# The first microseconds of a six-layer stack on one core: loading order, held loads and products of ones

## The chip, the cores and the metric

The kernel is one program on one NeuronCore of a Trainium2 chip. Its time is the device time of one execution in microseconds (us); lower is better. The span is the stretch from the first to the last instruction that the hardware profiler recorded in one such execution. Engines are named as in the profile: PE (matrix products; PEld are its weight loads), DVE (vector engine), ACT (scalar engine), POOL (GpSimd), SP (the engine that here only issues transfers). ACTq and SPq are those engines' instruction queues, POOLq the transfers that POOL issues.

## The reference, cut to what matters

A residual of 272 tokens (16 learned ones and 256 of the input) by 1024 features passes four layers (attention, mLSTM, HGRN2, attention) and then two layers of a second block. Only the entry into layer 0 bears on the change:

```python
u = rmsnorm(h, norm_gain[i])                       # h: 272 x 1024, fp32
q, k, v, z = _split(u @ w_in, (A_W, A_KVW, A_KVW, A_W))   # w_in: 1024 x 2560, fp32
q = rope(rmsnorm(q.reshape(bsz, lp, A_HEADS, A_HD), q_gain), pos)
k = rope(rmsnorm(k.reshape(bsz, lp, A_KV, A_HD), k_gain), pos)
...
h = h + jnp.where(valid[None, :, None], y, 0.0)
```

All inputs are fp32, and the products are to be of fp32 quality.

## The kernel before, in words

**Products in three passes.** Each fp32 operand is split into a rounded part (`hi`, the type fp32r) and the rest (`lo`). A block of 128 by 128 weights costs three products: hi by hi (L397), hi by the residual's lo (L398), lo by the residual's hi (L399). The residual's two halves are `XH` (written by ACT, L540) and `XL` (DVE, L528), one pair of instructions for each of the eight blocks k of 128 features; the residual itself, `HT`, comes in four transfers of two blocks each.

**Weights in parts.** The weights of the whole program lie in one array in the order of use and are read in parts of 128 partitions by 1024 columns (512 KB), which are eight blocks and so 24 products. I number the parts of layer 0 from 0. A part gets its two halves in one of two ways:
- *raw*: SP loads it to `wraw` (L258, three buffers), ACT rounds it to `whi` (L384), DVE subtracts to `wlo` (L390). Parts 0 to 5 of layer 0 go this way; parts 4 and 5 into the buffers MH and ML in place of whi and wlo.
- *by POOL*: POOL issues a transfer that rounds on its way into `whi` (L330, the "rounding load"), ACT writes its negative to `wlo` (L339), and POOL issues a second transfer of the same weights that adds onto it (L340). Parts from 6 on go this way. The rounding load is issued five parts ahead (`HI_AHEAD`), the second one three parts ahead (`LO_AHEAD`); `whi` has seven buffers, `wlo` five.

**The start.** SP issues, in this order, the small constants `sm`, HT blocks 0-1, part 0, HT 2-3, HT 4-5, part 1, HT 6-7, then tables of constants (`ce` with the rotary tables, `ca`), part 2, further tables, part 3 (L262, L258, `PRE`). POOL issues the rounding load of part 6 at once. ACT loads its table, makes XH and the squares `nsq` of the norm (L475), POOL adds the squares (`nsa`, L486), and two products with ones (L490, L491) give the sum for every token. The output tile of part 0 needs all eight blocks of XH and XL. The instructions are put in order on each engine by a scheduling layer that goes by the program's order and its own idea of when data are there; `Flow` (class `Flow`) places the attention's steps between the products by counted units of work.

**What follows the start.** Tile 0 (part 0) is a key tile, tiles 1 to 4 are queries. Their results pass ACT (square L690 or L737, scaled copy L692 or L740), a swap of halves by two transfers that ACT issues (`sw`, L589), DVE (rotary products L746 to L748) and the norm of the heads (L700, L702 and the Newton steps L440 to L444). At the middle of part 8 stand the short scores of the 16 learned tokens (L789), which wait for the last rotated queries (L748).

**Weights of later layers.** As soon as a raw buffer is free, SP loads the next raw part, which after part 5 belongs to layer 1.

Of the kernel before, what the change touches and what calls it, by code (L numbers as in the profile page):

```python
# [18 lines left out]
P = 128  # L19
# [29 lines left out]
PRE = (0, 4)  # L49
# [174 lines left out]
def kernel(ctx: ExitStack, tc: tile.TileContext, xt: bass.AP, pos: bass.AP, small: bass.AP,  # L224
# [19 lines left out]
    seq = order or _tile_order()  # L244
    acc = {}
# [5 lines left out]
    def load_raw(c0, n):  # L251

        t, kt, nt = seq[state["i"]]
        w = _cols(kt, nt)
        acc["nraw"] = acc.get("nraw", 0) + 1
        own = acc["raws"] if t[0] in "fd" and acc["nraw"] % 2 and "raws" in acc else wp
        raw = own.tile([P, SUB * P], F32, name="wraw", bufs=WR)
        nc.sync.dma_start(raw[:, :n], wts[state["off"]:state["off"] + P * w].rearrange("(p c) -> p c", p=P)[:, c0:c0 + n])  # L258
        return raw

    for k in range(0, KD, 2):
        nc.sync.dma_start(HT[:, k:k + 2, :], xt[:, k:k + 2, :])  # L262
        if stages[0] == 0 and len(raws) < len(PRE) and k == PRE[len(raws)]:
            raws.append(load_raw(len(raws) * SUB * P, SUB * P))
# [59 lines left out]
    def begin_parts(p):  # L324

        while parted and parted[0][0] <= p:
# [3 lines left out]
            nc.gpsimd.dma_start(hi[:, :c1 - c0], src)  # L330
# [23 lines left out]
    def chunk(tag, into=None, more_due=False):  # L354
# [6 lines left out]
        for c0 in range(0, n, SUB * P):  # L361
# [5 lines left out]
            if not more_due:  # L367
                begin_parts(p + HI_AHEAD)
# [3 lines left out]
            raw = raws.pop(0) if raws else load_raw(c0, c1 - c0)  # L372
# [8 lines left out]
            with ExitStack() as es:  # L381
                if (tag, state["n"], c0 // (SUB * P)) in HELD and "last" in acc:
                    es.enter_context(tc.issue_after(acc["last"]))
                nc.scalar.copy(hi[:, :c1 - c0], raw[:, :c1 - c0])  # L384
            with ExitStack() as es:
                if more and "lo" in acc:
                    es.enter_context(tc.issue_after(acc["lo"]))
                elif tag[0] == "f" and (state["n"], c0) == CH and "R" in acc:
                    es.enter_context(tc.issue_after(acc["R"]))
                V.tensor_tensor(lo[:, :c1 - c0], raw[:, :c1 - c0], hi[:, :c1 - c0].bitcast(F32), op=ALU.subtract)  # L390
# [102 lines left out]
    def keep_warm(src, n):  # L493

        ps = mx("s")
        for _ in range(n):
            PE.matmul(ps[:, :P], ones, src[:, :P], start=True, stop=True)
# [95 lines left out]
    class Flow:  # L593
# [29 lines left out]
        def run(self, gen):  # L623
            for w in gen:
                self.unit(w)

# [1504 lines left out]
```

## Time and profile before

| | us |
|---|---|
| median of 3 runs | 1443.03 |
| the runs | 1437.77, 1443.72, 1443.03 |
| the profiled execution | 1443.98 |
| its span | 1442.2 |
| PE busy in the span | 1365.0 (95%) |
| DVE / ACT / POOL busy | 988.1 / 770.1 / 445.6 |
| first product of the span starts at | 10.61 |

Some 1.8 us of the profiled execution lie outside of its span. A time in a row of the timeline is counted from the span's start; the second figure is how long the instruction took, and the brackets tell for how long the engine had been idle and what ended that. A product that streams 272 columns is listed with its whole passage, but the next one starts 0.125 us later at the full clock of 2.4 GHz and 0.227 us later at half of it; the granted clock in the windows is 1.00 and 0.50 for these two. "DMA" is the mean busy share of the 16 transfer engines; because packets overlap it can pass 1.

### The profile page before, as it was taken

The numbers are of one execution on the slowest core, as the hardware profiler recorded it, in microseconds if no ns is written. First come the engines' busy times: TensorE is split into PE (matmuls) and PEld (weight loads), VectorE is DVE, ScalarE is ACT, GpSimd is POOL, SyncE is SP. The second block draws the span as 40 slices with busy tenths as digits, with TensorE's granted clock in tenths as the row PEclk, the third lists the DMA queues.
The fourth block names the chain that finished last, engine by engine and source line by source line (L and its number), as shares of the span: only waits on it lengthen the run. The fifth ranks groups of instructions, "written<-read, shape, count | busy, mean of one in ns | idle before, by whom it ended". The sixth has DMA issues, their size and how long they took to land.

```text
span 1442.2 us, 27480 instructions
## 1 busy us (share of the span) xinstructions
PE 1365.0 (95%) x10347; PEld 1268.9 (88%) x10347; DVE 988.1 (69%) x2419; ACT 770.1 (53%) x1621; POOL 445.6 (31%) x611
## 2 busy tenths in 40 slices
PE   6999999999899999998999999999998998999998
PEld 5878999999899888897688888999998877899986
DVE  5765579999866666767655676787545665677754
ACT  5576655556635455455764656454444555455432
POOL 3222378778605333132214512100005430400000
PEclk9999999999999999999999999999999999999999
DMA  9988999999469988469879963566557975366662
GB/s 299 280 183 206 238 251 250 240 235 239 123 199 238 233 180 187 117 199 263 198 158 260 274 168 95 161 203 192 179 185 201 245 189 139 93 192 195 193 190 88
DMA packets 85493, 287.03 MB, mean 199 GB/s; under 512 B 10368, under 2 KB 16200, under 8 KB 85360
## 3 DMA queue, kind: packets, MB, share of 16 engines
q0 software_dynamic: 44512, 160.74, 48.2%
q1 hardware_dynamic: 34272, 118.60, 25.6%
q10 hardware_dynamic: 6576, 5.94, 1.5%
q8 instruction: 81, 1.33, 0.4%
q14 instruction: 52, 0.43, 0.1%
HBM read 279.01 MB, written 1.07 MB: 194 GB/s over the span
## 4 chain that ended last, share of the span: by engine, by line
PE 68%; DVE 13%; DMA 9%; ACT 4%; issue 3%; POOL 2%; ACTq 0%; DVEq 0%; SPq 0%; POOLq 0%
PE pmm L397 14%; PE pmm L398 13%; PE pmm L399 13%; DVE wlo L390 2%; PE ps L399 2%; PE ps L398 2%; PE ps L397 2%; DMA sw<-qg 2%; DMA wraw<-in_wts_dram 2%; DMA wlo<-in_wts_dram 2%; DMA sw<-qr 1%; DMA whi<-in_wts_dram 1%; PE pa L873 1%; PE ps L833 1%; DMA sw<-krr 1%
## 5 line engine op out<-in xcount | busy, mean ns | idle before, releaser
L397 PE MATMUL pmm<-XH,whi 128*128 128x272 f32 (+1 forms) x1544 | 460.3, 299 | 23.0 <-ACT whi L384 10.6
L398 PE MATMUL pmm<-XL,whi 128*128 128x272 f32 (+1 forms) x1544 | 447.2, 290 | 3.0 <-DVE XL L528 3.0
L399 PE MATMUL pmm<-XH,wlo 128*128 128x272 f32 (+1 forms) x1544 | 447.1, 290 | 2.4 <-DMA wlo<-in_wts_dram 1.9
L384 ACT CAST whi<-wraw 128x1024 fp32r<-128x1024 f32 (+1 forms) x211 | 218.0, 1033 | 237.9 <-DMA wraw<-in_wts_dram 195.9
L397 PEld LDWEIGHTS pmm<-XH,whi 128*128 128x128 f32 x1544 | 296.7, 192 | 36.8 <-ACT whi L384 10.6
L390 DVE TENSOR_TENSOR wlo<-wraw,whi 128x1024 fp32r<-128x1024 f32 (+1 forms) x211 | 256.2, 1216 | 87.7 <-PE pmm L399 36.1
L398 PEld LDWEIGHTS pmm<-XL,whi 128*128 128x128 f32 x1544 | 297.1, 192 | 4.6 <-DVE XL L528 4.0
L399 PEld LDWEIGHTS pmm<-XH,wlo 128*128 128x128 f32 x1544 | 297.2, 193 | 3.4 <-DMA wlo<-in_wts_dram 2.1
L339 ACT ACTIVATE wlo<-whi 128x1024 fp32r<-128x1024 f32 (+1 forms) x150 | 157.9, 1054 | 91.1 <-PE pmm L399 46.3
L330 POOL DMA_DIRECT2D whi<-in_wts_dram x150 | 88.5, 591 | 342.8 <-PE pmm L399 292.2
L397 PE MATMUL pmm<-MH,whi 128*128 128x256 f32 (+1 forms) x624 | 183.3, 294 | 0.6 <-DVE HT L961 0.6
L340 POOL DMA_DIRECT2D wlo<-in_wts_dram x150 | 130.2, 871 | 164.3 <-ACT wlo L339 93.4
L398 PE MATMUL pmm<-ML,whi 128*128 128x256 f32 (+1 forms) x624 | 179.2, 287 | 1.5 <-DVE ML L581 0.9
L399 PE MATMUL pmm<-MH,wlo 128*128 128x256 f32 (+1 forms) x624 | 178.4, 286 | 0.0
L397 PEld LDWEIGHTS pmm<-MH,whi 128*128 128x128 f32 x624 | 119.0, 191 | 7.9 <-issue 6.5
L398 PEld LDWEIGHTS pmm<-ML,whi 128*128 128x128 f32 x624 | 119.0, 191 | 2.2 <-DVE ML L581 1.1
L399 PEld LDWEIGHTS pmm<-MH,wlo 128*128 128x128 f32 x624 | 119.3, 191 | 0.0
L398 PE MATMUL ps<-XL,whi 128*128 128x256 f32 (+1 forms) x256 | 72.9, 285 | 0.0
L399 PE MATMUL ps<-XH,wlo 128*128 128x256 f32 (+1 forms) x256 | 72.5, 284 | 0.0
L397 PE MATMUL ps<-XH,whi 128*128 128x256 f32 (+1 forms) x256 | 72.3, 284 | 0.0
L528 DVE SCALAR_TENSOR_TENSOR XL<-HT,sm,XH 128x272 fp32r<-128x272 f32 (+1 forms) x64 | 35.3, 562 | 21.2 <-ACT XH L540 21.2
L399 PEld LDWEIGHTS ps<-XH,wlo 128*128 128x128 f32 x256 | 48.7, 190 | 0.3 <-DVE wlo L390 0.3
(927 smaller groups left out, 2854.2 us busy)
## 6 DMA issues: line engine op xcount, KB each, us to landing
wraw<-in_wts_dram SPq DMA_DIRECT2D x209, 512.0 KB, 4.5
whi<-in_wts_dram POOLq DMA_DIRECT2D x148, 512.0 KB, 6.5
wlo<-in_wts_dram POOLq DMA_DIRECT2D x148, 512.0 KB, 7.8
wraw<-in_wts_dram SPq DMA_DIRECT2D x16, 384.0 KB, 3.3
nb<-drb POOLq DMA_DIRECT2D x8, 272.0 KB, 5.5
HT<-in_xt_dram SPq DMA_DIRECT2D x4, 272.0 KB, 8.0
sw<-qg ACTq DMA_DIRECT2D x16, 68.0 KB, 6.6
sw<-qg ACTq DMA_DIRECT2D x16, 64.0 KB, 6.9
```

The source lines that it names most:

```text
L330: nc.gpsimd.dma_start(hi[:, :c1 - c0], src)
L339: act(lo[:, :w], hi[:, :w].bitcast(F32), AF.Copy, scale=-1.0)
L340: nc.gpsimd.dma_start(lo[:, :w], src, accum_op=ALU.add)
L384: nc.scalar.copy(hi[:, :c1 - c0], raw[:, :c1 - c0])
L390: V.tensor_tensor(lo[:, :c1 - c0], raw[:, :c1 - c0], hi[:, :c1 - c0].bitcast(F32), op=ALU.subtract)
L397: PE.matmul(ps, c.hi(b), xh, start=first, stop=False)
L398: PE.matmul(ps, c.hi(b), xl, start=False, stop=False)
L399: PE.matmul(ps, c.lo(b), xh, start=False, stop=last)
L528: acc["lo"] = V.scalar_tensor_tensor(XL[:, k, t0:], HT[:, k, t0:], smc(g, gi + k), XH[:, k, t0:].bitcast(F32), op0=ALU.mult, op1=ALU.subtr ...
L833: PE.matmul(sv, qp[:, n, qs], kp[:, :, k0:k1], start=True, stop=False)
L873: PE.matmul(po[64 * x:64 * x + 64, :], vt[:kk, bq - 1 + y, 64 * x:64 * x + 64], pT[:kk, y, x].rearrange("p n t -> p (n t)"), start=y == 0, ...
```

## The change: what it does

It touches the start of layer 0 alone; behind the first third of that layer the order of the instructions is the same on every engine.

1. **Steps.** Part 0 is loaded in four steps of 256 columns (`START = 2` blocks, 128 KB each), and rounded and subtracted in the same four steps.
2. **Order and queue of the residual.** HT 4-5 and 6-7 are issued by ACT as its first instructions; SP issues sm, HT 0-1, the first step, HT 2-3, three steps, then parts 1 and 2, and the tables of constants behind all of these.
3. **Held rounding loads.** The rounding loads that were issued before part 0 was prepared (`begin_parts` in `chunk`) are now issued behind a one-element POOL copy that reads the last element of part 0's `wlo` (`acc["begun"]`, `tc.issue_after`).
4. **Products of ones.** `keep_warm(ones, COLD)` puts eleven 128 by 128 products of a tile of ones in front of PE's work; their result is not read.

```diff
-PRE = (0, 4)
+START, COLD = 2, 11
...
-    def load_raw(c0, n):
+    def load_raw(c0, n, skip=0, step=SUB * P):
...
-        nc.sync.dma_start(raw[:, :n], wts[state["off"]:state["off"] + P * w].rearrange("(p c) -> p c", p=P)[:, c0:c0 + n])
-        return raw
-
-    for k in range(0, KD, 2):
-        nc.sync.dma_start(HT[:, k:k + 2, :], xt[:, k:k + 2, :])
-        if stages[0] == 0 and len(raws) < len(PRE) and k == PRE[len(raws)]:
-            raws.append(load_raw(len(raws) * SUB * P, SUB * P))
+        o = state["off"] + skip * P * w
+        src = wts[o:o + P * w].rearrange("(p c) -> p c", p=P)[:, c0:c0 + n]
+        for x in range(0, n, step):
+            nc.sync.dma_start(raw[:, x:min(n, x + step)], src[:, x:min(n, x + step)])
+            yield raw
+
+    def load_x(k, eng):
+        eng.dma_start(HT[:, k:k + 2, :], xt[:, k:k + 2, :])
+
+    load_x(0, nc.sync)
+    if stages[0] == 0:
+        load_x(4, nc.scalar)
+        load_x(6, nc.scalar)
+        one = load_raw(0, SUB * P, step=START * P)
+        raws.append(next(one))
+        load_x(2, nc.sync)
+        for _ in one:
+            pass
+        for x in range(1, WR):
+            raws += load_raw(x % 2 * SUB * P, SUB * P, skip=x // 2)
...
-            nc.gpsimd.dma_start(hi[:, :c1 - c0], src)
+            with ExitStack() as es:
+                if "begun" in acc:
+                    es.enter_context(tc.issue_after(acc.pop("begun")))
+                nc.gpsimd.dma_start(hi[:, :c1 - c0], src)
...
-            if not more_due:
+            if not more_due and p:
                 begin_parts(p + HI_AHEAD)
...
-            raw = raws.pop(0) if raws else load_raw(c0, c1 - c0)
+            raw = raws.pop(0) if raws else next(load_raw(c0, c1 - c0))
+            steps = [(c0, c1)] if p else [(x, x + START * P) for x in range(0, c1, START * P)]
...
+            for x0, x1 in steps:
+                x0, x1 = x0 - c0, x1 - c0
...
+                    nc.scalar.copy(hi[:, x0:x1], raw[:, x0:x1])
...
+                    V.tensor_tensor(lo[:, x0:x1], raw[:, x0:x1], hi[:, x0:x1].bitcast(F32), op=ALU.subtract)
+            if p == 0:
+
+                acc["begun"] = G.tensor_copy(mid[:, 3:4], lo[:, c1 - 1:c1].bitcast(F32)).ins
...
+    if stages[0] == 0:
+        keep_warm(ones, COLD)
```

How the instructions move, at three places. **ACT, the start of layer 0** (XH is the rounded residual, nsq its squares, whi the rounded weights). Before:

```order
L277 ACT_TABLE_LOAD
L277 ACTIVATE mid<-mid 128x1
L540 ACTIVATE XH<-HT,sm 128x272 x2
L475 ACTIVATE nsq<-HT 128x272 x2
L384 CAST whi<-wraw 128x1024
L540 ACTIVATE XH<-HT,sm 128x272 x2
L475 ACTIVATE nsq<-HT 128x272
L540 ACTIVATE XH<-HT,sm 128x272 x2
L475 ACTIVATE nsq<-HT 128x272 x2
L384 CAST whi<-wraw 128x1024
```

With the change:

```order
L265 DMA HT<-in_xt_dram 128x544 x2
L293 ACT_TABLE_LOAD
L293 ACTIVATE mid<-mid 128x1
L565 ACTIVATE XH<-HT,sm 128x272 x4
L500 ACTIVATE nsq<-HT 128x272 x2
L565 ACTIVATE XH<-HT,sm 128x272 x2
L406 CAST whi<-wraw 128x256
L565 ACTIVATE XH<-HT,sm 128x272 x2
L500 ACTIVATE nsq<-HT 128x272
L406 CAST whi<-wraw 128x256
L500 ACTIVATE nsq<-HT 128x272 x2
L406 CAST whi<-wraw 128x256 x2
```

Six of the eight XH (by the waits of the built program blocks 4-5, 0-1, 6-7 in this order) now stand in front of the first rounding of weights, where two stood before. Behind the last row shown come two nsq, the rounding of parts 1 and 2 and the last nsq.

**SP, its first transfers.** Before:

```order
L242 DMA sm<-in_small_dram 128x277
L262 DMA HT<-in_xt_dram 128x544
L258 DMA wraw<-in_wts_dram 128x1024
L262 DMA HT<-in_xt_dram 128x544 x2
L258 DMA wraw<-in_wts_dram 128x1024
L262 DMA HT<-in_xt_dram 128x544
L283 DMA ce<-in_cst_dram 128x856
L291 DMA ca<-in_cstb_dram 128x264
L258 DMA wraw<-in_wts_dram 128x1024
```

With the change:

```order
L242 DMA sm<-in_small_dram 128x277
L265 DMA HT<-in_xt_dram 128x544
L261 DMA wraw<-in_wts_dram 128x256
L265 DMA HT<-in_xt_dram 128x544
L261 DMA wraw<-in_wts_dram 128x256 x3
L261 DMA wraw<-in_wts_dram 128x1024 x2
L299 DMA ce<-in_cst_dram 128x856
```

Part 2 moved ahead of the tables; part 3 (not shown) moved from ahead of the last table to behind all of them.

**POOL, up to the second transfer of part 6** (whi from in_wts_dram is a rounding load, wlo from it the second transfer of a part, nsa the sum of squares). Before:

```order
L330 DMA whi<-in_wts_dram 128x1024
L486 ISA
L486 TENSOR_TENSOR nsa<-nsq 128x272
L486 TENSOR_TENSOR nsa<-nsq,nsa 128x272
L330 DMA whi<-in_wts_dram 128x1024
L486 TENSOR_TENSOR nsa<-nsq,nsa 128x272 x4
L330 DMA whi<-in_wts_dram 128x1024
L340 DMA wlo<-in_wts_dram 128x1024
```

With the change:

```order
L511 ISA
L511 TENSOR_TENSOR nsa<-nsq 128x272
L511 TENSOR_TENSOR nsa<-nsq,nsa 128x272 x3
L415 COPY mid<-wlo 128x1
L349 DMA whi<-in_wts_dram 128x1024 x3
L511 TENSOR_TENSOR nsa<-nsq,nsa 128x272 x2
L349 DMA whi<-in_wts_dram 128x1024 x2
L359 DMA wlo<-in_wts_dram 128x1024
```

The rounding loads of parts 6, 7 and 8 stand together behind the copy, and those of parts 9 and 10 stand ahead of part 6's second transfer, where before they stood behind it.

## Rows read from the trace of the kernel before

**Rows 1.** Who PE waited for, 0 to 150 us: total, times, longest.

```profile
PE pmm L397 <- ACT whi L384: 10.6, 1, 10.6
PE pmm L398 <- DVE XL L528: 2.0, 1, 2.0
PE ps L789 <- DVE qp L748: 1.7, 2, 0.9
```

**Rows 2.** Timeline, ACT and its queue, the start: start, took, instruction, count.

```profile
4.84 0.94 ACT L540 ACTIVATE XH<-HT,sm 128x272 fp32r<-128x272 f32 x2 [2.61 <-DMA HT<-in_xt_dram]
5.69 0.73 ACT L475 ACTIVATE nsq<-HT 128x272 f32<-128x272 f32 x2
9.52 1.04 ACT L384 CAST whi<-wraw 128x1024 fp32r<-128x1024 f32 x1 [3.10 <-DMA wraw<-in_wts_dram]
...
20.00 1.16 ACTq L589 DMA_DIRECT2D sw<-kg  x2
```

**Rows 3.** Timeline, DVE: the subtraction of a part's lo.

```profile
10.59 1.23 DVE L390 TENSOR_TENSOR wlo<-wraw,whi 128x1024 fp32r<-128x1024 f32 x1 [4.28 <-ACT whi L384]
...
15.36 1.79 DVE L390 TENSOR_TENSOR wlo<-wraw,whi 128x1024 fp32r<-128x1024 f32 x1
```

**Rows 4.** Timeline, PE: first product, part 1, part 4.

```profile
10.61 0.60 PE L397 MATMUL pmm<-XH,whi 128*128 128x272 f32 x1 [10.61 <-ACT whi L384]
...
18.90 0.43 PE L397 MATMUL pmm<-XH,whi 128*128 128x272 f32 x1
19.12 0.43 PE L398 MATMUL pmm<-XL,whi 128*128 128x272 f32 x1
...
30.67 0.29 PE L397 MATMUL ps<-XH,MH 128*128 128x272 f32 x1
```

**Rows 5.** Windows: stretch, length, busy of five engines, clock, DMA, GB/s.

```profile
2.00:9.00 7.00, 0.00 (x0) 0.00 (x0) 1.09 (x3) 1.79 (x6) 0.78 (x2) 1.00 0.95 280
9.00:16.00 7.00, 4.95 (x19) 4.20 (x19) 5.41 (x6) 6.48 (x15) 3.95 (x5) 1.00 1.04 401
16.00:24.00 8.00, 6.02 (x33) 5.73 (x32) 3.61 (x4) 2.58 (x4) 3.65 (x5) 0.79 0.91 282
24.00:70.00 46.00, 43.00 (x326) 38.85 (x324) 36.82 (x113) 27.45 (x66) 13.60 (x19) 0.96 1.09 287
```

**Rows 6.** DMA issues of 0.7 to 1.7 us: count, KB, us to landing.

```profile
sm<-in_small_dram SPq DMA_DIRECT2D x1, 138.5 KB, 2.2
HT<-in_xt_dram SPq DMA_DIRECT2D x1, 272.0 KB, 3.6
wraw<-in_wts_dram SPq DMA_DIRECT2D x1, 512.0 KB, 7.8
```

**Rows 7.** DMA issues: HT 2-3 (2.12 us), HT 4-5 with it (2.60), part 3 (12.07).

```profile
HT<-in_xt_dram SPq DMA_DIRECT2D x1, 272.0 KB, 7.9
...
HT<-in_xt_dram SPq DMA_DIRECT2D x2, 272.0 KB, 8.0
...
wraw<-in_wts_dram SPq DMA_DIRECT2D x1, 512.0 KB, 6.9
```

**Rows 8.** DMA issues of 28.21 and 31.54 us, second transfers of parts 7 and 8.

```profile
wlo<-in_wts_dram POOLq DMA_DIRECT2D x1, 512.0 KB, 10.8
...
wlo<-in_wts_dram POOLq DMA_DIRECT2D x1, 512.0 KB, 13.2
```

**Rows 9.** Timeline, PE: first use of lo in parts 7 and 8, short scores.

```profile
41.40 0.28 PE L398 MATMUL pmm<-XL,whi 128*128 128x272 f32 x1
41.52 0.29 PE L399 MATMUL pmm<-XH,wlo 128*128 128x272 f32 x1
...
45.30 0.29 PE L399 MATMUL pmm<-XH,wlo 128*128 128x272 f32 x1
...
48.85 0.23 PE L789 MATMUL ps<-kp,qp 128*16 128x32 f32 x2 [0.95 <-DVE qp L748]
```

**Rows 10.** Groups by line, 900 to 1100 us: eight products of ones, two records each.

```profile
L497 PE MATMUL ps<-nsl,ones 128*128 128x128 f32 x16 | 1.9, 275 | 0.0
```

More of the change, by code (lines that the diff above doesn't have):

```diff
@@ L243 @@
     HT = cp.tile([P, KD, T], F32, name="HT")
-    seq = order or _tile_order()
-    acc = {}
+    seq, acc = order or _tile_order(), {}
     state = {"i": 0, "off": 0, "n": 0, "p": 0}
@@ L257, in load_raw @@
         raw = own.tile([P, SUB * P], F32, name="wraw", bufs=WR)
-        nc.sync.dma_start(raw[:, :n], wts[state["off"]:state["off"] + P * w].rearrange("(p c) -> p c", p=P)[:, c0:c0 + n])
-        return raw
-    for k in range(0, KD, 2):
-        nc.sync.dma_start(HT[:, k:k + 2, :], xt[:, k:k + 2, :])
-        if stages[0] == 0 and len(raws) < len(PRE) and k == PRE[len(raws)]:
-            raws.append(load_raw(len(raws) * SUB * P, SUB * P))
+        o = state["off"] + skip * P * w
[16 more added lines that the diff above has]
+            raws += load_raw(x % 2 * SUB * P, SUB * P, skip=x // 2)
+    else:
+        for k in range(2, KD, 2):
+            load_x(k, nc.sync)
     def smc(name, i, n=1):
@@ L380, in chunk @@
                 lo = wp.tile([P, SUB * P], F32R, name="wlo", bufs=WB)
[L381 to L390, printed above, removed]
+            for x0, x1 in steps:
+                x0, x1 = x0 - c0, x1 - c0
+                with ExitStack() as es:
+                    if (tag, state["n"], c0 // (SUB * P)) in HELD and "last" in acc:
+                        es.enter_context(tc.issue_after(acc["last"]))
+                    nc.scalar.copy(hi[:, x0:x1], raw[:, x0:x1])
+                with ExitStack() as es:
+                    if more and "lo" in acc:
+                        es.enter_context(tc.issue_after(acc["lo"]))
+                    elif tag[0] == "f" and (state["n"], c0) == CH and "R" in acc:
+                        es.enter_context(tc.issue_after(acc["R"]))
+                    V.tensor_tensor(lo[:, x0:x1], raw[:, x0:x1], hi[:, x0:x1].bitcast(F32), op=ALU.subtract)
+            if p == 0:
+                acc["begun"] = G.tensor_copy(mid[:, 3:4], lo[:, c1 - 1:c1].bitcast(F32)).ins
             c.parts.append((hi, lo))
```

## The prediction

> **What bounds the kernel now.** I read the waits of PE first: over the first 150 us PE waits once for 10.6 us, until ACT has rounded part 0, then 2.0 us for XL, and 1.7 us at the short scores [rows 1]; for a transfer it never waits there. PE is busy for 95% of the span, and the order of work behind the start is unchanged, so what PE gains early can reach the end, unless something that does not move with PE takes it back. So the question has two halves: how much earlier PE can run through parts 0 to 4, and whether the weights behind them arrive earlier too.
>
> For the first half I read ACT's timeline: it is idle until the first HT has landed, makes one pair of XH (0.94 us) and of squares (0.73), then idles again for 3.1 us for part 0's weights and rounds them in 1.04 [rows 2]. PE's rows show part 1 under way at 18.90 and part 4 at 30.67 [rows 4]. At full clock a product takes 0.125 us (41.40 to 41.52 [rows 9]) and a part of 24 thus 3.0; parts 0 to 3 are 12.0 us of products and took from 10.61 to 30.67, 20.1. Part 1's rows stand 0.22 apart [rows 4], half clock: the wait for XL had let the clock fall, and in 16 to 24 us the granted clock is 0.79 [rows 5].
>
> For the second half I read the windows: the transfer engines are full from 2 to 9 us (0.95, but 280 GB/s), in 9 to 16 (1.04, 401 GB/s) and in 24 to 70 (1.09); only 16 to 24 is slack, 0.91 [rows 5]. And I compared the landing of the second transfers with their use: part 7's is issued at 28.21 and lands 10.8 later [rows 8], at 39.0, PE's first lo product of part 7 is at 41.52 [rows 9]: 2.5 us of slack. Part 8's lands at 31.54 + 13.2 = 44.7 [rows 8] and is used at 45.30 [rows 9]: 0.6 us of slack, and behind it PE waits 1.7 us for DVE anyway [rows 1], last until 48.85 [rows 9].
>
> **The change, part by part.**
>
> *Loads.* Before the first rounding ACT needs sm, three HT transfers and the first step: 138.5 + 3 x 272 + 128 KB, 1.11 MB. The first bytes flow at about 2 us (sm, alone on the engines, needed 2.2 from its issue at 0.74 [rows 6]). At the 280 GB/s of 2 to 9 us [rows 5] that is 4.0 us, at the 401 of the next window 2.8. The share of POOL's load is gone, but the packets are smaller; I take 4.0, with half a microsecond for the tail, so HT 4-5 lands at 4.4 (before, the first HT landed at 1.18 + 3.6 = 4.8 [rows 6]), HT 0-1 at 5.5, HT 6-7 and the first step at 6.4 to 6.7. The bound from above is today's: 512 KB of weights took 7.8 us behind sm and one HT [rows 6]. ACT's two issues cost 1.16 in front of its table load (from the sw pair [rows 2]); the first HT lands later than that, so it covers them.
>
> *ACT.* It is now one unbroken chain: two pairs of XH with 0.1 of waiting, a pair of squares, a third pair of XH: 4.4 + 3 x 0.94 + 0.73 + 0.1 = 8.1; a 256-wide rounding costs between a quarter of 1.04 and half of the XH pair [rows 2], I take 0.4: **PE starts at 8.5** instead of 10.61 [rows 4]. Then XH 2-3 (0.94), five squares (1.85), three roundings (1.2) and part 1 (1.04): done at 13.5. DVE's subtraction of part 1 takes 1.23 to 1.79, the longer one beside POOL's sums [rows 3]: about 15.0. DVE's last step of part 0 is done by 12.5, and PE ends part 0 before 14 at either clock, since it follows the steps.
>
> *Products.* With the clock up, parts 1 and 2 take 3.0 each from 15.0, the two sums of squares some 1.0 (a product with ones takes 1.9/8 = 0.24 for 128 columns [rows 10], 0.5 for 272), part 3 ends at 25.0. Eleven products of ones take 11 x 1.9/8 = 2.6 us at full clock [rows 10], up to twice that at half clock; nothing waits for PE then, so they cost nothing, and they end before 8.5.
>
> *Part 3 and 4.* Part 3's raw load is issued when DVE has freed part 0's buffer (12.5; at 12.07 before) and now queues behind all tables: 6.9 us before [rows 7], I take 6 to 7 as there is no rounding load ahead of it: 19, rounded 20, subtracted 21.3, in time. Part 4 is tighter, by ACT's queue: rounding of part 3 until 20, two sw issues 1.16, square and copy 0.8 (a pair of squares is 0.73), then the negative of part 6, square and copy again, the negative of part 7 and the rounding of part 4, the full-width ones 1.04 each like the rounding [rows 2]: 25.9, and DVE 1.23 more. PE so begins part 4's lo at 27 and the part in effect at 26.3, against 30.67: **4.4 us ahead** with the clock up; with half clock through part 1 two of them are lost.
>
> *Held loads.* Part 6's rounding load moves from 1.3 to about 13, parts 7 and 8 with it to 14 and 14.5 (each issue 0.6), behind a copy of 0.1. Behind the copy on POOL wait two nsa sums; the sum for all tokens needs them at 21, so they are covered. The second transfer of part 6 follows ACT's negative, about 23 (21.23 before); it is used some 7 us after part 4 begins, at 33. Parts 9 to 12 are issued 5 to 7 us earlier than before, as PE frees their buffers earlier. Cover is there until part 7.
>
> *What the weights give back.* Up to part 8's second transfer the same bytes must come: HT, tables, six raw parts, three of layer 1, seven rounding loads, three second transfers. The engines were full, so the landing moves ahead only by what was slack: 0.7 us (9% of the 8 us in 16 to 24) and what the first stretch gains by running faster than 280 GB/s: nothing to 7 x (1 - 280/401) = 2.1 us [rows 5]. That is 0.7 to 2.8; small steps take some of it back; I take **1.2**, nearer to the low end, because nothing shows which part of the slow stretch was POOL's doing. Part 7 can then be used 2.5 + 1.2 = 3.7 us earlier than now, less than the 4.4 that PE has; part 8 by 0.6 + 1.7 + 1.2 = 3.5, since the wait at the scores shrinks by what part 8 waits. DVE's chain to the scores starts from a product in part 7 and moves with it. Every later load is issued when PE frees a buffer, so it moves along. So **3.6 us** arrive at the end; bounds 2 (half clock, no slack gained) and 6.5 (weights no bound, and the half clock that 24 to 70 still holds, 4% of 46 us [rows 5], 1.8, gone with the wait that causes it).
>
> From the profiled execution, 1443.98, that is 1440.4; it stands 0.95 above the median of the three runs, and the median goes to **1439.4**.
>
> **The rivals.**
>
> *A. The weights do not move at all* (13%). The engines are full, and smaller packets eat what slack there was. Then part 7 allows 2.5 and part 8 2.3, less a clock that falls in longer waits: 1 to 2 us, 1441.5 to 1442. For it: 1.09 in 24 to 70 [rows 5]. Against: four rounding loads come earlier into a stretch that had room.
>
> *B. The weights are no bound* (19%). If the transfers speed up to 401 GB/s as soon as POOL's load is out, PE keeps 4.4 to 5.5 us and the 1.8 us of half clock shrink: 5.5 to 7.5, 1435.5 to 1437.5. For it: 401 GB/s with the same kind of transfers [rows 5]. Against: 280 GB/s also in parts of the later stretch.
>
> *C. Slower: the held load comes late* (9%). Part 6's rounding load was out of the way by 9.3; now it and four others stand ahead of part 6's second transfer in POOL's one queue. Two more loads ahead of it at 287 GB/s [rows 5] are 3.7 us. If part 7's second transfer lands later than 41.5, or part 8's later than 45.3 + 1.7 = 47.0, PE is behind today's. At 3.7 later part 8 lands at 48.4: 1.4 us lost, and with the clock falling in that wait up to 1.8 more: 1446. Against: parts 6 to 8 together are the same bytes as before, and their issues from part 9 on are earlier.
>
> *D. The products of ones do nothing* (10%). The order shows that they are issued, but they end by 6 and the first real product comes at 8.5; before, a wait of 2.0 us was enough for the next products to fall to half clock [rows 1, 4]. Parts 0 and 1 then run at 0.227 until the clock rises again; part 0 hides behind the roundings, part 1 loses up to 2.4, and PE is 2 to 3 ahead at part 4, 1441. The Trainium skill (TensorE: Matmul & The Clock Gate, Part 1) makes the low clock the default, which activity lifts and an idle stretch brings back; by that rule this is what would happen, and only the products of part 0 themselves, spread over 5 us, would warm PE for part 1. The trace agrees in that PE's first products ran at half clock; no run here shows products of ones followed by a pause.
>
> *E. The steps pay a fixed price each* (6%). If the landing of one step had to wait out the one before, four times 2.2 us (what sm needed, of the same size [rows 6]) would put the last step at 11 and the end of part 0 near 14.5 to 16; part 1's rounding behind it would follow by 1 to 2 us, and PE would be 2 to 3 ahead at part 4: 1441. Against: two HT transfers issued 0.48 apart took 7.9 and, with it in the median, 8.0 [rows 7], so they landed about as far apart as they were issued. The Trainium skill (DMA: Bandwidth & Descriptors, section Bandwidth) says to batch transfers to 1 MiB or more and calls those under 64 KB dominated by descriptors; by it the steps of 128 KB are the wrong way, and the trace bears it out only as far as 280 GB/s goes for small packets.
>
> **How the numbers follow.** My forecast has 43%. A measurement of this kernel can hardly tell less than 0.5%, 7.2 us, from no change: the three runs alone span 6. Faster by more needs the upper end of B or luck in the runs: 0.14. Slower by more needs C at more than twice its price: 0.05. The rest, 0.81, is within. The range holds the forecast's own bounds (2 to 6.5 us gained: 1436.5 to 1441), A, B, D and E, with a margin of 1.5 at the low and 2.5 at the high end for the scatter of the runs: 1434.0 to 1444.5. C is left out.
>
> **What would show it.** First product of layer 0 near 8.5, part 0 ended by 14, part 1's products 0.125 apart from 15, part 4's lo near 27; part 7's and 8's second transfers landing near 37.8 and 43.5, and PE waiting at these (L424), or at the short scores, less than 2 us each. Short scores done at 45 instead of 48.85, and the same distance kept at the end of layer 0 and of the span. Wrong would be: no wait for a second transfer and a shift of 5 or more; a shift at the scores under 1; a shift there that is gone later, which would name a bound that does not move with PE.

## The result, and the profile after

The change made the kernel slower. The median of five runs is 1454.17 us (1448.75 to 1457.89) beside 1438.61 of five runs of the kernel before (1433.85 to 1443.72): a ratio of 1.010, 95% interval 1.0062 to 1.0138. Measured again (e5, below) it was 1452.33 beside 1441.56, 1.0066, interval 1.0040 to 1.0092. So 0.7 to 1.0%, 10 to 14 us, are lost where 3.6 were to be gained.

| | before | after |
|---|---|---|
| profiled execution, us | 1443.98 | 1454.17 |
| its span | 1442.2 | 1452.4 |
| PE busy | 1365.0 | 1371.3 |
| first product of layer 0 | 10.61 | 8.22 |

The start went as forecast. PE's timeline after, the rows that answer to [rows 4]: first product, end of part 0, part 1, part 4:

```profile
8.22 0.40 PE L422 MATMUL pmm<-XH,whi 128*128 128x272 f32 x1 [2.45 <-ACT whi L406]
...
14.28 0.43 PE L424 MATMUL pmm<-XH,wlo 128*128 128x272 f32 x1
14.51 0.43 PE L422 MATMUL pmm<-XH,whi 128*128 128x272 f32 x1
...
17.72 0.29 PE L423 MATMUL pmm<-XL,whi 128*128 128x272 f32 x1
17.85 0.29 PE L424 MATMUL pmm<-XH,wlo 128*128 128x272 f32 x1
...
24.90 0.30 PE L422 MATMUL ps<-XH,MH 128*128 128x272 f32 x1
```

Part 4 begins 5.8 us earlier than in [rows 4]. Part 1 begins at half clock (0.23 apart) and ends at full clock (0.13). Then the lead goes. The six longest waits of PE after, 0 to 150 us, beside [rows 1]; the kernel before had one more of such a size, which [rows 1] leaves out, 1.8 us for ACT (pT) in the attention behind the scores:

```profile
PE pt L886 <- DVE rt L467: 3.3, 1, 3.3
PE pmm L422 <- ACT whi L406: 2.4, 1, 2.4
PE pmm L424 <- DMA wlo<-in_wts_dram: 2.2, 1, 2.2
PE ps L861 <- ACT p__667 L873: 1.8, 1, 1.8
PE ps L817 <- DVE qp L776: 1.5, 1, 1.5
PE ps L522 <- DVE ones L287: 1.1, 1, 1.1
```

New are one wait for a transfer (2.2 us, part 7's second transfer) and two in the attention of layer 0, behind DVE and ACT (3.3 and 1.8). The second transfers of parts 6, 7 and 8, issued at 20.45, 24.12 and 26.94 us, answer to [rows 8], where parts 7 and 8 took 10.8 and 13.2 (the page's last part, a window around each issue):

```profile
wlo<-in_wts_dram POOLq DMA_DIRECT2D x1, 512.0 KB, 14.5
...
wlo<-in_wts_dram POOLq DMA_DIRECT2D x1, 512.0 KB, 16.6
...
wlo<-in_wts_dram POOLq DMA_DIRECT2D x1, 512.0 KB, 17.8
```

Parts 7 and 8 are issued 4.1 and 4.6 us earlier than before and land at 40.8 and 44.7 us, where before they landed at 39.0 and 44.7. The windows, beside [rows 5]:

```profile
2.00:9.00 7.00, 4.30 (x23) 3.89 (x21) 3.52 (x9) 5.62 (x14) 0.76 (x1) 0.98 0.96 341
9.00:16.00 7.00, 7.00 (x31) 6.68 (x32) 6.42 (x7) 4.84 (x12) 6.02 (x8) 0.53 0.97 312
16.00:24.00 8.00, 8.00 (x63) 7.84 (x62) 3.98 (x9) 5.37 (x10) 3.55 (x6) 1.00 1.04 345
24.00:70.00 46.00, 37.43 (x271) 32.82 (x269) 29.13 (x91) 20.83 (x49) 11.62 (x16) 0.96 1.09 284
```

The transfer engines are full from 2 to 70 us at about the rate of before. PE is busy for 37.4 of the 46 us from 24 to 70, where it was 43.0. The clock of 9 to 16 us is 0.53 here and 1.00 in [rows 5], but the kernel before did not run at full clock there: its profile has no record of the clock until 15.4 us, and its products at 14.95 and 15.18 us stand 0.23 apart, at half clock too.

To find where time goes I took the same product in two profiles and subtracted its start. At the end of layer 0's attention, before and after:

```profile
90.43 0.49 PE L858 MATMUL pt<-ce,p__974 128*128 128x128 f32 x3
```

```profile
94.25 0.49 PE L886 MATMUL pt<-ce,p__996 128*128 128x128 f32 x3
```

That is +3.8. The table gives this distance from the first profile of before (positive is behind it) for products that lie there at 30, 48, 90, 840, 920 and 1430 us, one profiled execution each, and the ratio of the times with its interval, from 8 to 12 runs each (5 for the change). One run of e17 (1458.48 us), over 1.5% above the fastest of its kernel, counts as slow and is not in its ratio.

| run | 30 | 48 | 90 | 840 | 920 | 1430 | ratio |
|---|---|---|---|---|---|---|---|
| the change | -5.8 | -0.5 | +3.8 | +10.2 | +16.7 | +10.4 | 1.010 (1.0062 to 1.0138) |
| e5 the change again | -5.1 | +1.1 | +6.8 | +8.2 | +15.3 | +8.4 | 1.0066 (1.0040 to 1.0092) |
| e12 before again | +1.8 | +1.8 | +3.5 | +3.5 | +3.5 | +0.2 | |
| e1 order back, one row | -6.8 | +0.3 | +4.3 | +6.0 | +12.3 | +8.7 | 1.0034 (1.0007 to 1.0061) |
| e9 order back | -6.8 | +0.5 | -1.2 | +4.3 | +11.4 | +4.6 | 1.0030 (1.0009 to 1.0050) |
| e3 order into before | -1.8 | -1.8 | +8.7 | +5.0 | +6.4 | +3.2 | 1.0065 (1.0041 to 1.0089) |
| e4 hold alone | -5.9 | -3.0 | +2.2 | +8.7 | +10.4 | +8.5 | 0.9998 (0.9973 to 1.0023) |
| e8 no hold | -2.8 | -1.6 | +7.3 | +11.2 | +17.3 | +10.2 | 1.0063 (1.0037 to 1.0088) |
| e6 raws held | -7.0 | -1.6 | +3.4 | +3.6 | +10.1 | +10.8 | 1.0035 (1.0009 to 1.0061) |
| e7 raws held, in before | -1.0 | -2.9 | -4.5 | +2.6 | +2.9 | -4.2 | 0.9980 (0.9954 to 1.0005) |
| e10 raws held, order back | -6.4 | -3.3 | -5.4 | -7.3 | -2.0 | -5.1 | 1.0010 (0.9985 to 1.0036) |
| e11 the same, no hold | -2.7 | -3.5 | -3.3 | +5.0 | +6.3 | +3.4 | 1.0015 (0.9991 to 1.0040) |
| e2 no ones | -5.8 | -0.9 | +5.3 | +5.3 | +5.8 | +3.5 | 1.0016 (0.9987 to 1.0045) |
| e15 = e9, no ones | -6.3 | +0.8 | -0.6 | -1.9 | -1.8 | -3.5 | 0.9992 (0.9972 to 1.0012) |
| e14 = e10, no ones | -5.2 | -4.1 | -5.3 | -5.5 | -5.0 | -9.1 | 0.9980 (0.9956 to 1.0005) |
| e13 ones into before | +0.8 | +1.1 | +0.2 | +3.6 | +10.5 | +7.3 | 1.0026 (0.9997 to 1.0056) |
| e17 five ones into before | -0.6 | -0.6 | 0.0 | -0.2 | +1.8 | -3.7 | 1.0006 (0.9981 to 1.0031) |
| e18 eleven ones, layer 3 | -1.3 | +0.6 | +2.3 | +5.5 | +11.6 | +5.5 | 1.0030 (1.0006 to 1.0053) |
| e16 hold, raws, order | -5.8 | -7.0 | -6.2 | -7.6 | -2.5 | -2.5 | 0.9969 (0.9947 to 0.9990) |

So the loss has three places: the lead of 5 to 6 us is gone by 48 us; 4 to 6 more are lost between 48 and 90; and 6 to 7 between 840 and 920, where the order of the work is the same. Between 90 and 840 us the change loses 6.4 more, but e5, the same kernel, 1.4; I can't name a cause there.

The profiled execution need not be a typical one: those of e4 and e6 took 9 and 7 us more than the median of their runs, those of e3, e10 and e14 some 5 less.

### The profile page after: what moved, and what is told of

Its sections match the earlier page's. It is cut to its first block, busy times and chain, and to the rows that moved or that the text cites. A ratio compares the mean times of both kernels' runs of the same rounds, so it can differ in the third digit from the quotient of the medians.

```text
span 1452.4 us, 27537 instructions
## 1 busy us (share of the span) xinstructions
PE 1371.3 (94%) x10369; PEld 1272.2 (88%) x10369; DVE 989.3 (68%) x2422; ACT 771.0 (53%) x1624; POOL 446.9 (31%) x612
## 3 DMA queue, kind: packets, MB, share of 16 engines
q8 instruction: 82, 1.34, 0.4%
## 4 chain that ended last, share of the span: by engine, by line
PE 65%; DVE 14%; DMA 11%; ACT 4%; issue 3%; POOL 2%; ACTq 0%; DVEq 0%; SPq 0%; POOLq 0%
PE pmm L422 13%; PE pmm L424 13%; PE pmm L423 13%; DMA sw<-qg 3%; DVE wlo L412 2%; PE ps L423 2%; PE ps L424 2%; PE ps L422 2%; DMA wlo<-in_wts_dram 2%; DMA wraw<-in_wts_dram 2%; DMA whi<-in_wts_dram 1%; PE ps L861 1%; DMA sw<-krr 1%; PE pa L901 1%; PE ps L1293 1%
## 5 line engine op out<-in xcount | busy, mean ns | idle before, releaser
L406 ACT CAST whi<-wraw 128x1024 fp32r<-128x1024 f32 (+2 forms) x214 | 218.0, 1021 | 235.8 <-DMA wraw<-in_wts_dram 188.4
L412 DVE TENSOR_TENSOR wlo<-wraw,whi 128x1024 fp32r<-128x1024 f32 (+2 forms) x214 | 259.1, 1214 | 87.2 <-PE pmm L424 38.6
L423 PEld LDWEIGHTS ps<-XL,whi 128*128 128x128 f32 x256 | 48.8, 191 | 0.0
```

The lines of the kernel that those rows point to most:

```text
L406: nc.scalar.copy(hi[:, x0:x1], raw[:, x0:x1])
L412: V.tensor_tensor(lo[:, x0:x1], raw[:, x0:x1], hi[:, x0:x1].bitcast(F32), op=ALU.subtract)
L423: PE.matmul(ps, c.hi(b), xl, start=False, stop=False)
```

## The experiments

My first theories were: **order** (in layer 0 the scheduling layer orders DVE and ACT otherwise, and that costs), **transfers** (the held loads come late), and **later** (something behind layer 0 belongs to the change).

**The same kernels again (e5, e12).** No edit.

> The changed kernel as it is, once more, beside the same runs of the kernel before as the next three. Theory 'order and transfers' (5 us of lead given back to late second transfers by 48 us, then 4 more to DVE's order): PE 3 to 5 us behind at 90 us again, and 1449 to 1451 where the kernel before shows 1445. Theory 'later' (a further loss behind layer 0 belongs to the change): the distance grows to about 10 us behind layer 0 again, above all near 676, 845 and 855 us, and the time is 1454 or more.

> A second profiled execution of the kernel before. If the differences of up to 6 us behind layer 0 (at 193, 676, 845, 855 and 1200 us) are scatter of single executions, two executions of the same kernel show them too, while they agree within 1 us up to 90 us.

The loss in layer 0 and the loss at 840 to 920 us came again in e5. Two executions of the kernel before were 3.5 us apart at 90 us, more than the 1 us I had expected, up to 5.8 between 200 and 720, and 3.5 again at 920; so a single distance is good to some 3 to 6 us, a loss within a short stretch is read more safely, and the ratios decide. Behind 920 us the distances shrink by up to 7 us without a pattern that I can name: at 1200 us PE waits 4.8 us for DVE in the first profile of before, 2.8 in the second and 0.8 in the change.

**Order.** DVE's timeline after, at the first scores of layer 0 (sta are the maxima, sw the rotation of a swapped query of the next head group):

```profile
55.03 0.44 DVE L775 TENSOR_TENSOR sw<-sw,ce 128x272 f32<-128x272 f32 x1 [2.52 <-DMA sw<-qg]
55.51 0.44 DVE L776 TENSOR_TENSOR qp<-qp,sw 128x272 f32<-128x272 f32 x1
55.87 0.45 DVE L866 TENSOR_REDUCE sta<-ps 128x2 f32<-128x288 f32 x1
58.75 0.44 DVE L775 TENSOR_TENSOR sw<-sw,ce 128x272 f32<-128x272 f32 x1 [2.43 <-DMA sw<-qg]
59.11 0.15 DVE L867 TENSOR_TENSOR sta<-sta,rqT 128x2 f32<-128x2 f32 x1
```

and in the kernel before:

```profile
54.72 0.45 DVE L838 TENSOR_REDUCE sta<-ps 128x2 f32<-128x288 f32 x1
55.20 0.16 DVE L839 TENSOR_TENSOR sta<-sta,rqT 128x2 f32<-128x2 f32 x1
55.39 0.16 DVE L840 TENSOR_TENSOR sta<-sta,nsk 128x2 f32<-128x2 f32 x1
55.59 0.16 DVE L841 TENSOR_TENSOR sta<-sta,nsk 128x2 f32<-128x2 f32 x1
55.67 0.44 DVE L747 TENSOR_TENSOR sw<-sw,ce 128x272 f32<-128x272 f32 x1
```

Before, all rows of the first maxima stood ahead of both rotations; after, the first row (L866) stands behind one rotation and the others behind both, so DVE waits twice for a swap (2.52 and 2.43 us) before ACT can begin the exponentials. And ACT's next swap is issued behind those. After, with the exponentials at 59.77 and the swap at 60.05:

```profile
56.13 1.06 ACT L358 ACTIVATE wlo<-whi 128x1024 fp32r<-128x1024 f32 x1
59.77 0.47 ACT L873 ACTIVATE p__667<-ps,sta,rqT 128x144 f32<-128x144 f32 x1 [2.58 <-DVE sta L868]
60.05 0.47 ACTq L614 DMA_DIRECT2D sw<-qg  x1
```

Before, with both 4.1 and 2.6 us earlier:

```profile
55.67 0.45 ACT L845 ACTIVATE p__645<-ps,sta,rqT 128x144 f32<-128x144 f32 x1
...
57.45 1.12 ACTq L589 DMA_DIRECT2D sw<-qg  x2
```

A late swap so makes the next one late. DVE's waits for swaps from 48 to 90 us, before, after and in e9:

```profile
DVE sw L747 <- DMA sw<-qg: 4.3, 3, 1.7
```

```profile
DVE sw L775 <- DMA sw<-qg: 10.4, 3, 5.4
```

```profile
DVE sw L775 <- DMA sw<-qg: 2.5, 4, 1.2
```

e1 puts the second rotation behind the maxima, e9 each one behind those of one scores step; e3 forces the reverse into the kernel before.

```diff
 e9: in attend.scores, layer 0
-                    V.tensor_sub(es, nm, n2)
+                    es_ = V.tensor_sub(es, nm, n2).ins
+                    acc["turned"] = [t for t in acc["turned"] if t[0] != hf]
+                    if i == 0 and acc["turned"]:
+                        tc.add_manual_dep(acc["turned"].pop(0)[1], es_.name, mybir.DependencyInfo(
+                            mybir.DependencyClass.NoSync, mybir.DependencyReason.DATA), reason="order")
 e3: in attend.scores and swap, layer 0 of the kernel before
+                    with tc.issue_after(acc.pop("turned")[1]):
+                        V.tensor_mul(nm, nm, rr)
...
+                with tc.issue_after(acc["exp"]):
+                    nc.scalar.dma_start(sw[d:d + n, c0:], src[s:s + n, c0:])
```

> The changed kernel, with the scheduler kept from putting DVE's rotation of a swapped query (L775) ahead of the rows that make the maxima of the scores (sta) in layer 0; SP, POOL and PE keep their order. Theory 'order': in the changed kernel these rows make DVE wait for the swap, ACT's exponentials wait for DVE and the next swap for ACT; the jumps of PE behind the kernel before at 59.4 (+2.0) and 67.2 us (+3.4) go, and PE is level or up to 1 us ahead at 75 us instead of 3.8 behind; the time falls by about 4, to 1450. Theory 'transfers': the loss is the late weights alone; then PE stays 3 to 4 us behind at 75 us and the time stays at 1454. Theory 'later': whatever happens in layer 0, 6 us or more are lost behind 380 us; then the time is still 1447 or more above where layer 0 puts it.

> The changed kernel with each swapped query's rotation in layer 0 put behind the maxima of one scores step, first with first, second with second, as they stood in the kernel before; e1 had left the first one ahead. PE, SP and POOL keep the changed kernel's order. Theory 'order': DVE then no longer waits for a swap in front of the maxima, the loss from 48 to 90 us falls from 4 to 6 us to under 1.5, PE at 90 us stands at 0 to +1.5 against the kernel before, and the time is within 2 us of it. Rival 'late swaps': the swaps themselves come late whatever stands in front; then 3 us or more are still lost there and the time stays 5 or more above.

> The kernel before, with two of its rows forced as they stand in the changed one: DVE's maxima of the scores (sta) in layer 0 behind the rotation of the swapped query, and the issue of the next swap behind ACT's first exponentials. Loads are untouched. Theory 'order': PE falls behind the kernel before by 3 to 7 us between 55 and 75 us and the time rises by as much, to 1442 to 1446. Theory 'transfers': no more than 1 us.

e1 missed: it still lost 4.0 us from 48 to 90, for the first rotation stood ahead as it had. With both put back (e9) PE gains 1.7 us there where the change loses 4 to 6. The other way round (e3) 10.5 us are lost in the kernel before, and the time rises by 0.65%, more than the 3 to 7 us expected; its edit also moved rows of PE, DVE and ACT at 901 to 944 and behind 1248 us, so not all of that need be layer 0. With e9, which moves nothing behind 82 us, the order is shown as a cause. In the time it is worth 0.36% (e5 to e9) or 0.24% (e2 to e15), about 4 us. But e9 was expected within 2 us of the kernel before and was still 0.3% slower, although PE is ahead at 90 us: order and transfers do not make up the whole.

**Transfers.** e4 adds the hold alone to the kernel before; e8 takes it out of the change; e6 holds the first three raw loads of layer 1 until the short softmax is done (e7 does so in the kernel before); e10 and e11 add e9's order.

```diff
 e8 (e11): no hold
-            if not more_due and p:
+            if not more_due:
                 begin_parts(p + HI_AHEAD)
...
-            if p == 0:
-                acc["begun"] = G.tensor_copy(mid[:, 3:4], lo[:, c1 - 1:c1].bitcast(F32)).ins
 e6 (e7, e10, e11): in load_raw, for three loads of layer 1; mid[:, 4] is written in turn0
+            nc.scalar.copy(raw[:, :1], mid[:, 4:5])
```

> The kernel before with the held rounding loads alone (one POOL copy of part 0's lo, the loads of parts 6 and on behind it); no steps, no ones, residual by SP. The scheduler then orders layer 0's attention much as in the changed kernel. Theory 'order': about 4 us lost between 55 and 75 us. Theory 'transfers': PE waits at parts 6 to 8 for second transfers, up to 3 us lost by 45 us. Both together: 1443 to 1447. If neither holds: 1438.

> The changed kernel with the rounding loads of parts 6 to 8 issued as early as before (no copy, no wait). Theory 'transfers': the second transfers of parts 6 and 7 land some 3 us earlier, PE does not wait at part 7, and 2 us more of the lead are kept at 48 us, less what the first steps lose to part 6's load in the first 9 us (up to 1 us). Theory 'order': the order of layer 0's attention is between the two kernels' (the first row of the maxima stands ahead of the swapped query's row, the second behind it), so 2 to 5 us are still lost between 55 and 75; time 1446 to 1450.

> The changed kernel, with the first three raw loads of layer 1 held back until an element of the short softmax has been copied (about 75 us); before, one of them stood ahead of part 6's second transfer and all three ahead of part 8's. Theory 'transfers': these 1.5 MB at 284 GB/s are 5.5 us of the stretch; part 7's second transfer then lands at 37 to 39 instead of 40.8 and part 8's at 40 to 42, and PE keeps 2 to 4 us more of its lead at 48 us. The scheduler's order in layer 0 moves again, so the attention behind it may still lose 2 to 5 us; time 1445 to 1448. If bandwidth is not what delays them: landing as before, 1450.

> The kernel before with the same three raw loads of layer 1 held back, nothing else. Theory 'transfers': PE does not wait for weights there, so nothing is gained by it, 1444 to 1446; only the swaps, which pass the same transfer engines, may land 1 to 2 us earlier. Theory 'order': the scheduler's order moves here too, and if it puts maxima behind swaps, 2 to 4 us are lost between 55 and 75 us.

> e6 (the changed kernel with layer 1's raw loads held back) with the same order forced. If transfers and order are the two takers: about 2 us of lead at 48 us as in e6, kept to 90 us (-2 to -1), and 1 to 2 us faster than the kernel before. If the order is not what took it in e6: +3 at 90 us again.

> The same, with the rounding loads of parts 6 to 8 not held back either: from the change there remain the steps, the order of the residual and the products of ones. Theory 'transfers': raws of parts 4 and 5 no longer share the engines with three rounding loads, the second transfers land as in e6 or earlier; lead of 2 to 4 us at 48 us and at 90 us; 2 to 4 us faster than the kernel before, within 0.3%.

e4 starts as early as the whole change. PE's first waits in e4:

```profile
PE pmm L402 <- ACT whi L387: 7.6, 1, 7.6
PE pmm L403 <- DVE XL L533: 0.9, 2, 0.7
```

10.6 of [rows 1] have become 7.6, by keeping one 512 KB load out of the first microseconds, without steps or a new order of the residual. The steps without the hold (e8) are 2.8 ahead at 30 us. But neither the hold alone nor taking it out changes the time: e4 stands at 0.9998, and e8 at 1.0063 beside e5's 1.0066. Both lose their lead in the attention, in the order that the scheduling layer made for them: 5.2 us from 48 to 90 in e4 and 8.9 in e8, where 4 and 2 to 5 were expected, with DVE waiting 9.9 and 10.6 us for swaps. In e6 the second transfers of parts 7 and 8, issued at 24.8 and 28.2 us, take

```profile
wlo<-in_wts_dram POOLq DMA_DIRECT2D x1, 512.0 KB, 11.9
...
wlo<-in_wts_dram POOLq DMA_DIRECT2D x1, 512.0 KB, 12.9
```

and land at 36.8 and 41.1 us, 3.6 to 4 earlier than in the change, about as expected: the raw loads of layer 1 stood in the way. In the change the first of them is issued at 19.3 us, at 27.8 before, since part 3's buffer comes free sooner; it is not needed before layer 1. The hold has a share in it: without it (e8) the first raw load is issued at 25.0, and parts 7 and 8 land as early as in e6, at 37.3 and 41.2. At 48 us e6 stood at -1.6 (the change at -0.5 and +1.1), 1 to 3 us more of the lead instead of 2 to 4, as PE waited 2.7 us for part 4's rounding (MH) there; e10 and e14 at -3.3 and -4.1.

In the time the held raw loads are worth 0.20% (e9 to e10) and 0.12% (e15 to e14), 2 us; small beside the intervals, but of one sign. The same holds for the 0.31% from e5 to e6, where the order in layer 0 moves too. In these three pairs the edit also moves rows of PE and ACT between 1121 and 1289 us. e7 shows that this gain is not all of late weights: the kernel before does not wait for them and was to gain nothing, but with the raw loads held its ratio is 0.9980 and its PE 4.5 us ahead at 90; the order of DVE and ACT moved there as well, from 40 us on, and I did not part the two. e10 and e11 were to be 1 to 4 us faster than the kernel before and came out at 1.0010 and 1.0015, although PE is ahead at 90: a loss behind layer 0 was still in them, and for e10 the next experiments show which.

**Products of ones.** e2, e14 and e15 set `COLD` to 0; e13 puts `keep_warm(ones, 11)` in front of the kernel before, e17 the same with 5, and e18 eleven of them ahead of layer 3's norm instead (at 589 to 603 us in its profile, not 650 as I had expected).

> The changed kernel without the eleven products of ones; the order on DVE, ACT, POOL and SP is unchanged. Theories 'order' and 'transfers' both give the products nothing: parts 0 and 1 ran at half clock with them as well, so first product at 8.2, part 4 at 25, and 1454 within the scatter. A theory 'ones' (they cost power or clock later, or put off the first product by waiting for the ones) would show a time 3 us or more lower and a granted clock that falls less often.

> The kernel before with the eleven products of ones in front, and nothing else; every engine but PE keeps its order. Theory 'ones cost later': PE is level with the kernel before through layer 0 (within its own 3 us of scatter), loses 5 to 7 us between 840 and 920 us, and the time rises by 3 to 5 us. Theory 'chance': the same time as before within 2 us, and a loss at 840 to 920 or at 1200 us as it falls.

> e10 (the changed kernel, layer 1's raw loads held back, order of layer 0 forced) without the products of ones. PE 4 to 6 us ahead at 90 us as in e10. 'Ones cost later': no loss between 840 and 920 us, and 2 to 4 us faster than the kernel before. 'Chance': as e10, 1 us slower to 1 us faster.

> e9 (the changed kernel with layer 0's order forced) without the products of ones. 'Ones cost later': level with the kernel before or 1 us faster. 'Chance': 3 to 5 us slower, as e9.

At the start they do nothing: without them (e2) PE's first product is at 8.34 instead of 8.22, full clock begins at 15.3 instead of 15.6, and PE is as far ahead at 30 us. Later they cost: five pairs that differ by them alone are 0.26 (e13), 0.30 (e18), 0.38 (e9, e15), 0.30 (e10, e14) and 0.50% (e5, e2) apart, 0.35% or 5 us in the mean, all of one sign; no pair alone is far outside of its interval.

Where it lies is seen in the table, 840 to 920 us. There, in layer 4, ACT issues a swap of keys (krr), and 1.17 us after its first half SP issues a raw load, in every profile. A swap is two transfers of 64 KB; by their bytes they are q10's packets here. Transfers of 2.8 us from the swap's issue, in the kernel before (issued at 840.16):

```profile
q0 software_dynamic: 90, 0.30, 55.0%
q10 hardware_dynamic: 160, 0.13, 17.1%
q1 hardware_dynamic: 21, 0.09, 14.1%
q14 instruction: 1, 0.01, 1.0%
...
sw<-krr ACTq DMA_DIRECT2D x2, 64.0 KB, 2.3
```

and in e13 (issued at 843.96):

```profile
q0 software_dynamic: 88, 0.29, 53.6%
q10 hardware_dynamic: 154, 0.13, 16.7%
q1 hardware_dynamic: 12, 0.05, 10.0%
q8 instruction: 1, 0.02, 2.0%
...
sw<-krr ACTq DMA_DIRECT2D x2, 64.0 KB, 4.0
```

A packet of queue q8 has come into the swap's flight, twice the size of the q14 packet before; there q8's came 4.5 us after the issue, when the swap had landed. The queue moves 81 packets, 1.33 MB together, in the whole run before and 82, 1.34 MB, with the eleven products:

```profile
q8 instruction: 81, 1.33, 0.4%
```

```profile
q8 instruction: 82, 1.34, 0.4%
```

That is 16 KB a packet. As PE has 20,738 weight loads and products after (the page's first part), 65 bytes for each, I read it as PE's instructions; the spacing bears this out: in each of the 20 profiles a packet comes every 255 to 256 of PE's weight loads and products in the mean.

The Trainium skill (Runtime: NRT & Kernel Launch, Instruction fetch mechanics) says that engines refill their instructions in blocks of 16 KiB by a queue of their own and calls the cost of crossing one mostly hidden. The sizes agree; what a crossing costs PE itself no run here shows. What the profiles show is the swap with a fetch in its flight. The eleven products of ones are 44 instructions (each is two weight loads and two products), by these figures 0.17 of a packet; a packet comes every 17 us, so the fetches should come some 3 us earlier, an estimate, and this one came 3.0 earlier.

In all ten profiles with eleven products the packet begins 1.2 to 1.8 us behind the swap's issue, and the swap's first half takes 3.2 to 3.9 us; in all ten without, or with five, it begins 4.0 to 5.1 behind, and the half takes 2.2 to 2.6. Everything behind the swap shifts, and the next swap (of queries, qr), whose second half was issued 0.97 us ahead of a raw load in the kernel before, is issued 0.24 ahead in e13 and takes 4.5 us instead of 2.0. DVE's waits for swaps in that stretch, 838 to 870 us before, 842 to 880 in e13:

```profile
DVE sw L1588 <- DMA sw<-krr: 1.5, 2, 0.8
...
DVE sw L1588 <- DMA sw<-qr: 0.3, 1, 0.3
```

```profile
DVE sw L1591 <- DMA sw<-qr: 3.5, 1, 3.5
...
DVE sw L1591 <- DMA sw<-krr: 2.8, 1, 2.8
```

> The kernel before with five products of ones in front instead of e13's eleven. Eleven moved the q8 packet from +4.5 to +1.5 us behind the swap's issue, 0.27 each, so five put it at about +3.1. 'Place of the instructions': the swap is through by then (2.1 to 2.6 us), no loss between 840 and 920 us, the time within 2 us of the kernel before. 'What the products do at the start': about half of e13's loss, 2 us, or the same loss at 840 to 920 us.

> The kernel before with eleven products of ones among the first products of layer 3 (about 650 us), none at the start. 'Place of the instructions': from there on as in e13, the packet at about +1.5 behind the swap's issue, the swap 3.4 to 4.7 us, 5 to 7 us lost between 840 and 920 us. 'What the products do at the start': no loss there. Either way up to 1 us for the products themselves.

e18 settles that the loss at 840 to 920 us comes with the place in PE's instructions and not with the start: the products stand some 590 us further on, and the packet is at +1.2, the swap takes 3.2, and 6 us are lost there. (Its ratio holds 2.5 us more, lost at 600 us where its products stand, beside the 1 us expected.) The number expected of e17 was wrong: its 20 instructions should by the same estimate have moved the packet by 1.3 us, but it stayed at +4.5, and why is open; with it there the swap took 2.5 and the time is that of the kernel before.

The second step, the race of the next swap with a raw load, is not the products' alone: e11 has the packet in the swap and loses 1.3 us, e16 has it not and loses 5.1. What differs is the lead of that swap's second half over the raw load: in the ten profiles with 0.05 to 0.24 us, e16's among them, it takes 4.4 to 4.8 us, in the ten with 0.33 (e11) to 1.0 us 2.0. Why one packet (18.7% of 16 engines in 0.3 us, so 0.9 us of one engine) costs a swap 1.3 us was not tried, and no run moved the packet alone.

**A kernel without the takers (e16).** The kernel before with the hold (e4), layer 1's raw loads held (e6) and e9's order; no steps, no ones, residual by SP.

> The kernel before with the held rounding loads, layer 1's raw loads held back and layer 0's order forced; no steps, no change to the residual's loads, no ones. e4 had PE 3 us ahead at 48 us with the hold alone; with 5.5 us of raw loads out of the way and the order forced it should be 4 to 6 us ahead at 90 us, and 3 to 5 us (0.2 to 0.35%) faster than the kernel before. If the steps and the early residual are needed for the lead: under 2 us.

It is 0.31% faster than the kernel before (1437.04 beside 1442.86, interval 0.1 to 0.5%), 4.5 us as expected, and the only one whose interval lies below 1. PE is 7.0 us ahead at 48 us and 6.2 at 90. The steps and the early residual are not needed for this: e14, which has them too, is at 0.9980. How much of it is the hold is open, as e7, without the hold, is at 0.9980 as well.

## Why the prediction was wrong

**Right: the start.** Part 4 is 5.8 us ahead where 4.4 were forecast; first product at 8.22 (8.5), part 0 ended at 14.4 (before 14), part 4's lo at 26.1 (27). That the products of ones would cost nothing there held, and so did rival D's mechanism: they did not keep the clock up; part 1 began at half clock and lost 0.4 us of 3.0 by it. What I did not see is that the hold alone (e4) does it. Rival E's fixed price for each step did not show: the four landed at 6.2, 7.7, 8.0 and 8.4 us. Nor did rival B's rate: with POOL's load out of the way 341 and 312 GB/s flowed up to 16 us, not 401.

**Wrong: "weights give back".** I took the landing of parts 7 and 8 as 1.2 us earlier, by a sum of bytes; part 7's came 1.7 later and part 8's as before. The bytes were counted as those that must come up to part 8, with three raw loads of layer 1 among them; when these come was left out. In the change all three land ahead of part 7's second transfer (30.3, 35.2 and 38.4 us beside 40.8); before, only the first did (34.2, 39.2 and 42.9 beside 39.0). e6 shows 3.6 to 4 us for them. Three rounding loads at 12.7 to 14 us stand in front of parts 4 and 5 besides. (The sum also took 3.6 where the smaller of its two bounds, 3.5, was the one that binds.) Of the 3.6 us that were to arrive at the end nothing was left at 48 us. This is rival C's mechanism at part 7, a wait of 2.2 us for a second transfer; alone it would have been worth little.

**Wrong, and with the next step what made the kernel slower: "the order of work behind the start is unchanged, so what PE gains early can reach the end".** PE's order is, but for the products with ones; that of DVE moves until 77 us and that of ACT until 74, and I costed none of it. The section on the change says that the order is the same behind the first third of layer 0; this layer lasts until about 135 us, so the order differs in more than its first half. It takes 6 to 8 us between 48 and 90 us (the change and e5 beside e9, e2 beside e15) and about 4 of the time. That DVE's chain to the scores "moves with it" holds for the short scores (48.0, 0.8 earlier than before), not for the scores behind them.

**Wrong: products of ones "cost nothing".** True up to 650 us (e13); about 5 us behind that, above all at 840 to 920, by a mechanism that no rival had: 44 more instructions of PE, as far as the profiles show it a fetch that falls into a swap, and a late next swap. It weighs as much as the order: with the order put back and the ones left in (e9) the kernel is 0.30% slower than before, with the ones out and the order left (e2) 0.16%, an interval that takes in no change, and with both mended (e15) it is level.

**The sum.** 5 us gained by 30 us, 5 given back by 48, then 4 for the order and 5 for the products: 9 behind, against 9.5 of e5's ratio and 14 of the first measurement, whose interval begins at 9. Each of the three terms is good to 2 or 3 us, so that they add up so closely is in part luck.

## What to carry to other kernels

Where a scheduling layer orders the engines, compare the whole order of every engine that a wait runs through, not the start alone, and price each row that has moved behind a transfer; a change of loads can reorder arithmetic 50 us further on. When loads are made to start earlier, ask which unneeded ones start earlier too. Dummy products should be tried without their purpose: take them out, and put them elsewhere; if the same stretch loses the same time, it is their place in the instructions.

## What the runs showed of the hardware

A fetch of PE's instructions stands among the packets of the transfer engines, 16 KB for every 255 to 256 weight loads and products, here every 17 us in the median. With 44 more instructions one fetch fell into a 64 KB swap: 2.2 to 2.6 us for its first half became 3.2 to 3.9. A swap whose second half was issued up to 0.24 us ahead of a 512 KB load took 4.4 to 4.8 us for that half, with 0.33 to 1.0 us of lead 2.0. Two executions of one kernel differ by up to 3.5 us within layer 0.
